# Rotary tables and latent norms moved from the end of the seven-product stage into its middle, in a hybrid mLSTM and latent-attention layer

## The chip, the cores and the metric

The kernel runs on one core of a Trainium2 chip. The metric is the time of one execution on the device in microseconds (us), as the median of several runs. TensorE (PE) does the matmuls, VectorE (DVE), ScalarE (ACT) and GpSimd (POOL) the elementwise work, and SyncE (SP) and ACT issue the DMA transfers. Each engine works through its own queue in order and waits at semaphores for the others.

## The reference

One layer with two branches that read the same normalised input, in float32, for 512 tokens of width 2048:

```
h     = rms_norm(x, norm_g)
q_a, k_a, v_a, o_a, i_a, f_a, z_a, c_q, c_kv, k_r, z_b, g_a, g_b = split(h @ w_in)
# branch A: causal conv + silu on q_a and k_a, then a gated matrix memory (mLSTM), 8 heads
y_a   = (sigmoid(o_a) * rms_norm(mlstm(q_a, k_a, v_a, i_a, f_a)) * silu(z_a)) @ w_a
# branch B: attention over low-rank latents, 16 heads of 128 + 64 (rotary) channels
q_b   = rms_norm(rms_norm(c_q, q_lat_g) @ w_uq)         # per head
k, v  = split(rms_norm(c_kv, kv_lat_g) @ w_ukv)
k_b   = rms_norm(concat(k, k_r))                        # k_r is shared by all heads
q_b, k_b: the last 64 channels turned by cos/sin(position * inv_freq)
y_b   = (causal_attention(q_b, k_b, v) * silu(z_b)) @ w_b
out   = x + (sigmoid(g_a) * y_a + sigmoid(g_b) * y_b) @ w_out
```

The latents c_q and c_kv are 512 wide each. What the change moves is the forming of the cos/sin tables, the rotary part of the shared key, and the root-mean-square norms of c_q and c_kv.

## The kernel before

**Products in split form.** Every float32 operand of a matmul is split into a high part that PE reads at its fast float32 form and a remainder. `split` does it in two instructions: ACT casts the high part, DVE subtracts it from the source (lines 104 to 106). A product then takes three matmuls: high by high, low by high, high by low.

**Stages.** (1) Three groups of columns of `w_in` are multiplied with h: the latents, the shared key and the mLSTM gates (`load_c`, `proj_tok`, `evac_c`). The raw latents are copied by ACT out of PSUM into `cc` tiles and written to DRAM (`cq_d`, `ckv_d`); 80 columns stay on the chip as `misc`. While the second and third group run, the list `later` is worked off one piece per weight tile: `build` normalises h (`normal`), splits it for the products to come (`parts`), and forms sums of its quarters (`combine`, `split_sums`). `parts` also sends the split upper half of h to DRAM (`htop_d`), two transfers on SP for each of eight row blocks: the spills.

(2) The seven-product stage (`strassen`): ten jobs of 1024 columns of `w_in` (o, z, g_a, g_b, v), each computed as a 2 x 2 block product with seven products instead of eight. A job has 28 steps, seven products (p = 0 to 6) of four, and a step is 12 matmuls. `prep` loads a weight block two steps ahead (`rx` or `rr`, SP) or subtracts two blocks (DVE, line 467), `part` splits the block one step ahead into `wh` (ACT) and `wl` (DVE, three and two buffers), `mult` issues the matmuls, and `finish` puts the output's sums into `later`, of which one piece runs per step. Outputs go through `tmp` tiles (six buffers, shared by many things) to DRAM on ACT's queue.

(3) Nine steps before the end of the last job, the pool of h's parts (`sap`) is closed, pools for the next stage are opened over it, and a generator, `early`, is advanced twice per step: it loads the raw latents back from DRAM (`latent`, `c` tiles, four loads of 512 KB), forms the rotary tables and the rotated key (`rope_setup`: about forty short DVE instructions on 128 x 128, and a dozen on POOL), then the norms of the latents (squares on ACT, inverse roots on POOL, scaling on DVE).

(4) The next stage begins with the silu gate of the first head pair (`pair_gate`, weights through `load_w`), woven with the transposes of the normalised latents into `lat`. Its weights come through `raw`, `whi` and `wlo` (4, 3 and 2 buffers). `ht`, the upper half of h, is loaded back from DRAM into the space of the stage that ends. Head pairs, mLSTM heads and output products follow.

**What sets the order.** The kernel is written as a program in one order; a planner then lists the instructions of each engine's queue by when it expects their inputs to be ready, and by program order where several are. It may put an instruction ahead of an earlier one. It inserts all semaphores. `tc.issue_after(i)` makes the instructions of a block that are on the engine of `i` stand behind `i` in the queue; `tc.add_manual_dep` does it for one instruction. Neither makes them wait for its end.

Of the kernel before, what the change touches and what calls it, by code (L numbers as in the profile page):

```python
# [19 lines left out]
P = 128  # L20
# [24 lines left out]
def hybrid_kernel(  # L45
# [207 lines left out]

    def evac_c(g):
# [50 lines left out]
    def build(j):  # L305
        f = whole[j]

# [14 lines left out]

        sums = []
# [10 lines left out]
        def split_sums():  # L334
            hi = sap.tile([P, 4, 256], F32R, tag=f"sh{j}", name=nm("sh"))
# [51 lines left out]
    def latent(i, src, gain):  # L387
# [3 lines left out]
        yield  # L391
        ss = small([P, T], "ssl")
        for t in range(T):
            A.activation(junk, c[t // 2][:, t % 2, :], AF.Square, accum_out=ss[:, t:t + 1])
        G.tensor_scalar(ss, ss, 1.0 / LORA, None, ALU.mult)
        ms = small([P, T], "msl")
        G.tensor_scalar(ms, msx, EPS, None, ALU.mult)
        G.tensor_tensor(ms, ms, ss, ALU.add)
        sc = small([P, T], "scl")
        rsqrt(sc, ms, T)  # L400
        for t in range(T):
            V.tensor_scalar(c[t // 2][:, t % 2, :], c[t // 2][:, t % 2, :], sc[:, t:t + 1], None, ALU.mult)
# [42 lines left out]
    def strassen(jobs, comb):  # L445
# [38 lines left out]
        def part(c, p, j):  # L484
# [3 lines left out]
            split(hi, lo, w)  # L488
# [60 lines left out]
        part(*steps[0])  # L549
        for n, s in enumerate(steps):  # L550
# [34 lines left out]
    def rope_setup():  # L585

        V.tensor_copy(pos_f, pos_i)
        ropes = big([P, 7, P], F32, "rope")
        angf, jq, z2, sn, cs, j4, qa = [ropes[:, a, :] for a in range(7)]
        ang = angf.rearrange("p (t f) -> p t f", t=T)  # L590
        for t in range(T):
            V.tensor_scalar(ang[:, t, :], freq, pos_f[:, t:t + 1], None, ALU.mult)
        MAGIC = 12582912.0
# [23 lines left out]
        for c in CC[1:]:  # L617
            V.scalar_tensor_tensor(cs, cs, c, z2, ALU.add, ALU.mult)
        V.tensor_scalar(cs, cs, 1.0, None, ALU.add)
# [3 lines left out]
        V.scalar_tensor_tensor(j4, j4, -4.0, jq, ALU.mult, ALU.add)  # L623
        V.tensor_tensor(qa, j4, j4, ALU.mult)
        V.tensor_scalar(qa, qa, -1.0, 1.0, ALU.mult, ALU.add)
        V.tensor_scalar(qa, qa, -1.0, None, ALU.max)
        yield
        qb = jq
        V.tensor_tensor(qb, qa, qa, ALU.mult)
        V.tensor_scalar(qb, qb, -1.0, 1.0, ALU.mult, ALU.add)  # L630
        V.tensor_tensor(qb, qb, j4, ALU.mult)
        sc_t = big([P, 2, P], F32, "rope")
        sinf, cosf = sc_t[:, 0], sc_t[:, 1]
# [6 lines left out]
        V.tensor_tensor(z2, cs, qb, ALU.mult)  # L640
        V.tensor_tensor(sinf, sn, qa, ALU.mult)
        V.tensor_tensor(sinf, sinf, z2, ALU.add)

# [12 lines left out]
        rk = big([P, 4, T, DR], F32, "rk")  # L656
        rka, rkb = rope_tables(gkr, rk[:, 0:2])

        kr, krt = rk[:, 2], rk[:, 3]
        for t in range(T):  # L660
            V.tensor_scalar(kr[:, t, :], misc[:, t, 0:64], r[:, t:t + 1], None, ALU.mult)
        for t in range(T):
            A.activation(junk[:, :DR], kr[:, t, :], AF.Square, accum_out=ssr[:, t:t + 1])
        G.tensor_tensor(krope, kr, rka, ALU.mult)
        G.tensor_tensor(krt[:, :, 0:32], kr[:, :, 32:64], rkb[:, :, 0:32], ALU.mult)
        G.tensor_tensor(krt[:, :, 32:64], kr[:, :, 0:32], rkb[:, :, 32:64], ALU.mult)
# [4 lines left out]
    def early():  # L671
        for i, (src, gain) in enumerate(((cq_d, qlg), (ckv_d, kvlg))):
            lats.append(latent(i, src, gain))
            next(lats[i])
        yield
        for _ in rope_setup():
            yield
        for lat in lats:
            next(lat)
            yield  # L680


    lats, side = [], None
    last = 28 * len(jobs) - 9
    for n, _ in enumerate(strassen(jobs, comb_h)):
        if n == last:
# [3 lines left out]
            side = early()  # L690
        if side is not None:
            for _ in range(2):
                next(side, None)
    while later:
        run_later()
    drain(side)
# [579 lines left out]
```

## Time and profile before

| | us |
|---|---|
| median of three runs (2143.95 to 2147.92) | 2143.98 |
| profiled execution, its own time | 2141.43 |
| its span, first to last instruction | 2139.7 |
| PE busy | 2105.3 (98%) |
| DVE busy | 1398.0 (65%) |
| ACT busy | 982.9 (46%) |
| POOL busy | 172.5 (8%) |

All times inside the span are us from its start. The mean granted clock of TensorE is 0.998 of full speed. Stage (1) runs to about 121.7, the seven-product stage from 124.4 to about 904, its second job from 203.6 to 279.8. Lines (L106) are those of the kernel before; L105 and L106 are the two halves of every split, so tiles tell which one it is. A busy PE is not PE at its peak, and a "<-" in brackets names what ended the idle time before an instruction.

### The profile page before, as it was taken

The numbers are of one execution on the slowest core, as the hardware profiler recorded it, in microseconds if no ns is written. First come the engines' busy times: TensorE is split into PE (matmuls) and PEld (weight loads), VectorE is DVE, ScalarE is ACT, GpSimd is POOL, SyncE is SP. The second block draws the span as 40 slices with busy tenths as digits, with TensorE's granted clock in tenths as the row PEclk, the third lists the DMA queues.
The fourth block names the chain that finished last, engine by engine and source line by source line (L and its number), as shares of the span: only waits on it lengthen the run. The fifth ranks groups of instructions, "written<-read, shape, count | busy, mean of one in ns | idle before, by whom it ended". The sixth has DMA issues, their size and how long they took to land.

```text
span 2139.7 us, 28857 instructions
## 1 busy us (share of the span) xinstructions
PE 2105.3 (98%) x10200; PEld 1781.2 (83%) x10200; DVE 1398.0 (65%) x2260; ACT 982.9 (46%) x2025; POOL 172.5 (8%) x306
## 2 busy tenths in 40 slices
PE   8999999999999999899999999999999999999999
PEld 8888888888888888688888888788878878888889
DVE  6877778787786788856666666766785433443233
ACT  8544444444444444445555555545564322222221
POOL 0000000000000000222222222201111000000000
PEclk9999999999999999999999999999999999999999
DMA  6746425524633643642222222275563543332443
GB/s 165 174 163 197 130 87 177 168 94 132 194 104 103 191 147 106 206 126 79 81 84 76 80 77 82 81 229 151 165 229 126 182 143 98 112 130 94 137 130 118
DMA packets 205313, 286.01 MB, mean 134 GB/s; under 512 B 31217, under 2 KB 111473, under 8 KB 204145
## 3 DMA queue, kind: packets, MB, share of 16 engines
q1 hardware_dynamic: 189040, 256.90, 39.6%
q10 hardware_dynamic: 16128, 27.27, 3.6%
q8 instruction: 80, 1.31, 0.3%
q14 instruction: 65, 0.52, 0.1%
HBM read 240.07 MB, written 44.04 MB: 133 GB/s over the span
## 4 chain that ended last, share of the span: by engine, by line
PE 92%; DMA 2%; DVE 2%; ACT 2%; issue 1%; POOL 1%; SPq 0%; ACTq 0%; DVEq 0%; POOLq 0%
PE acc L114 16%; PE acc L113 16%; PE acc L115 16%; PE acc L512 8%; PE acc L513 8%; PE acc L511 7%; PE aux L512 4%; PE aux L513 4%; PE aux L511 4%; PE aux L113 2%; PE aux L115 2%; PE aux L114 2%; ACT junk L236 1%; PE aux L840 1%; PE aux L800 1%
## 5 line engine op out<-in xcount | busy, mean ns | idle before, releaser
L106 DVE TENSOR_TENSOR wlo<-raw,whi 128x512 fp32r<-128x512 f32 (+3 forms) x432 | 285.4, 663 | 388.4 <-PE acc L114 279.9
L105 ACT CAST whi<-raw 128x512 fp32r<-128x512 f32 (+3 forms) x432 | 259.2, 601 | 526.5 <-PE acc L115 356.2
L106 DVE TENSOR_TENSOR wl<-rx,wh 128x1024 fp32r<-128x1024 f32 x160 | 196.6, 1229 | 114.2 <-PE aux L512 64.7
L105 ACT CAST wh<-rx 128x1024 fp32r<-128x1024 f32 x160 | 168.9, 1055 | 177.4 <-PE acc L513 106.7
L114 PE MATMUL acc<-wlo,g 128*128 128x512 f32 x512 | 200.1, 391 | 2.8 <-DVE wlo L106 2.7
L113 PE MATMUL acc<-whi,g 128*128 128x512 f32 x512 | 200.1, 394 | 2.7 <-ACT whi L105 1.6
L115 PE MATMUL acc<-whi,g 128*128 128x512 f32 x512 | 199.5, 390 | 0.8 <-DVE g L106 0.8
L105 ACT CAST wh<-rr 128x1024 fp32r<-128x1024 f32 x120 | 126.5, 1054 | 160.7 <-PE aux L513 88.1
L106 DVE TENSOR_TENSOR wl<-rr,wh 128x1024 fp32r<-128x1024 f32 x120 | 146.5, 1221 | 27.5 <-PE aux L512 14.6
L511 PE MATMUL acc<-wh,sh 128*128 128x512 f32 x400 | 155.6, 389 | 0.0
L512 PE MATMUL acc<-wl,sh 128*128 128x512 f32 x400 | 155.6, 389 | 0.0
L513 PE MATMUL acc<-wh,sl 128*128 128x512 f32 x400 | 155.6, 389 | 0.0
L114 PEld LDWEIGHTS acc<-wlo,g 128*128 128x128 f32 x512 | 96.2, 188 | 24.3 <-DVE wlo L106 5.4
L113 PEld LDWEIGHTS acc<-whi,g 128*128 128x128 f32 x512 | 95.9, 188 | 22.0 <-ACT whi L105 1.8
L115 PEld LDWEIGHTS acc<-whi,g 128*128 128x128 f32 x512 | 96.0, 188 | 21.2 <-DVE g L106 1.2
L113 PE MATMUL acc<-whi,y 128*128 128x512 f32 (+1 forms) x320 | 111.1, 348 | 0.0
L115 PE MATMUL acc<-whi,y 128*128 128x512 f32 (+1 forms) x320 | 111.0, 347 | 0.0
L114 PE MATMUL acc<-wlo,y 128*128 128x512 f32 (+1 forms) x320 | 111.0, 347 | 0.0
L113 PE MATMUL acc<-ht,whi 128*128 128x512 f32 x256 | 101.5, 397 | 0.0
L113 PE MATMUL acc<-h8h,whi 128*128 128x512 f32 x256 | 101.1, 395 | 0.0
L115 PE MATMUL acc<-h8h,wlo 128*128 128x512 f32 x256 | 100.2, 392 | 0.3 <-DVE wlo L106 0.3
L114 PE MATMUL acc<-h8l,whi 128*128 128x512 f32 x256 | 100.4, 392 | 0.0
(357 smaller groups left out, 5041.6 us busy)
## 6 DMA issues: line engine op xcount, KB each, us to landing
rr<-in_w_in SPq DMA_DIRECT2D x120, 512.0 KB, 4.8
raw<-in_w_in SPq DMA_DIRECT2D x128, 256.0 KB, 2.8
rx<-in_w_in SPq DMA_DIRECT2D x40, 512.0 KB, 5.1
raw<-in_w_b SPq DMA_DIRECT2D x64, 256.0 KB, 3.1
raw<-in_w_a SPq DMA_DIRECT2D x64, 256.0 KB, 3.0
raw<-in_w_out SPq DMA_DIRECT2D x64, 256.0 KB, 3.1
raw<-in_w_ukv SPq DMA_DIRECT2D x32, 256.0 KB, 2.8
raw<-in_w_uq SPq DMA_DIRECT2D x32, 192.0 KB, 2.4
```

The lines of the kernel that those rows point to most:

```text
L105: A.copy(dst_hi, src)
L106: return V.tensor_tensor(dst_lo, src, f32(dst_hi), ALU.subtract)
L113: PE.matmul(ps, lh, rh, start=start, stop=False)
L114: PE.matmul(ps, lh, rl, start=False, stop=False)
L115: PE.matmul(ps, ll, rh, start=False, stop=stop)
L236: A.activation(junk[:, :P], xr[:, t, :], AF.Square, accum_out=ssx[:, k, t:t + 1])
L511: PE.matmul(out[i], lh[:, tok], hi[:, n, :], start=first, stop=False, skip_group_check=cont)
L512: PE.matmul(out[i], lh[:, tok], lo[:, n, :], start=False, stop=False, skip_group_check=cont)
L513: PE.matmul(out[i], ll[:, tok], hi[:, n, :], start=False, stop=k == H8 - 1, skip_group_check=cont)
L800: PE.transpose(ps[:, t * P:(t + 1) * P], src(t), ident)
L840: PE.transpose(ps[:, j * P:(j + 1) * P], pr[:, j * P:(j + 1) * P], ident)
```

## The change

- **The first weights ahead of the copies.** The four `cc` copies of the third column group must stand behind the first `wh` cast of the seven-product stage in ACT's queue.
- **Spills later.** The two transfers to `htop_d` of a row block are issued in `split_sums`, two pieces of `later` after `parts`.
- **`rope_setup` and the norms leave the end.** From step 28 on, one piece per step of a chain is run: first `rope_setup`, cut into pieces of one to five DVE instructions, then `normalised` for c_q and for c_kv. A block around each piece queues its ACT and DVE instructions behind the latest `wh` and `wl` (`marks`). The chain must be through by nine steps before the end.
- **Borrowed storage.** The tables no longer take `big` tiles, which exist only at the end; they are formed in `rB` (the spread inverse norms, used up by then), `wg_raw` (the gate weights, used up) and the result tiles `rq` and `krope`.
- **Through DRAM.** `normalised` reads each raw latent back in pieces of 256 KB into `tmp` tiles, once for the squares and once more to scale them, and writes the scaled pieces over the raw ones. That is 16 loads and 8 stores on SP. `latent` then loads normalised values, at the same place as before, and only transposes and splits them.
- **`hold`.** The first three splits of the next stage's weights queue behind the last `wh` and `wl` on ACT and DVE.

```diff
     def split(dst_hi, dst_lo, src):
-        A.copy(dst_hi, src)
-        return V.tensor_tensor(dst_lo, src, f32(dst_hi), ALU.subtract)
+        hi = A.copy(dst_hi, src)
+        lo = V.tensor_tensor(dst_lo, src, f32(dst_hi), ALU.subtract)
+        return hi, lo
...
+    hold, marks = [0], []
+
+    def behind_parts(stack):
+        for i in marks:
+            stack.enter_context(tc.issue_after(i.ins))
...   # load_w
-                low[0] = split(hi, lo, raw)
+                with ExitStack() as held:
+                    if hold[0]:
+                        hold[0] -= 1
+                        behind_parts(held)
+                    low[0] = split(hi, lo, raw)[1]
...   # evac_c
-            A.copy(cc, ps)
+            copy = A.copy(cc, ps)
+            if g == 2:
+                copies.append(copy)
...   # build: parts, split_sums
-                SP.dma_start(htop_d[j][:, :, n:n + 256], f32(dst))
+                spills.append((htop_d[j][:, :, n:n + 256], f32(dst)))
...
         def split_sums():
+            for spill in spills:
+                SP.dma_start(*spill)
...   # latent: squares, inverse roots and scaling go
...   # strassen: part, and ahead of the steps
-            split(hi, lo, w)
+            marks[:] = split(hi, lo, w)
...
         part(*steps[0])
+        for i in copies:
+            tc.add_manual_dep(i.ins, marks[0].ins.name, in_turn, reason="first weights before the copies")
...   # rope_setup: more yields, other storage
-        ropes = big([P, 7, P], F32, "rope")
-        angf, jq, z2, sn, cs, j4, qa = [ropes[:, a, :] for a in range(7)]
+        jq, z2, sn, cs = [rB[:, a * P:(a + 1) * P] for a in range(4)]
+        angf, cosf = [wg_raw.rearrange("p k c -> p (k c)")[:, a * P:(a + 1) * P] for a in range(2)]
+        j4, qa = [rq[:, 0].rearrange("p t f -> p (t f)")[:, a * P:(a + 1) * P] for a in range(2)]
...
+    def normalised(src):
+        def piece(t):
+            x = tmp(512, "lx")
+            SP.dma_start(x, src[t // 2][:, t % 2, :])
+            return x
+        ss = small([P, T], "ssl")
+        for t in range(T):
+            x = piece(t)
             yield
+            yield
+            A.activation(junk, x, AF.Square, accum_out=ss[:, t:t + 1])
...   # ms, sc: inverse roots on POOL, as before
+        for _ in range(4):
+            yield
+        for t in range(T):
+            x = piece(t)
+            yield
+            yield
+            V.tensor_scalar(x, x, sc[:, t:t + 1], None, ALU.mult)
+            yield
+            SP.dma_start(src[t // 2][:, t % 2, :], x)
...
+    side = chain(rope_setup(), normalised(cq_d), normalised(ckv_d))
     last = 28 * len(jobs) - 9
     for n, _ in enumerate(strassen(jobs, comb_h)):
         if n == last:
             close_pool("sap")
             wpool[0] = open_pool("wp")
             big_pool.extend((None, (open_pool("bpa"), NB_A)))
-            side = early()
-        if side is not None:
-            for _ in range(2):
+            for lat in lats:
+                next(lat)
+        elif n >= 28:
+            with ExitStack() as held:
+                behind_parts(held)
                 next(side, None)
+    hold[0] = 3
     while later:
         run_later()
-    drain(side)
```

## Rows read from the trace of the kernel before

**Rows 1.** The page, engines: busy us, share of the span, instructions.
```profile
PE 2105.3 (98%) x10200; PEld 1781.2 (83%) x10200; DVE 1398.0 (65%) x2260; ACT 982.9 (46%) x2025; POOL 172.5 (8%) x306
```

**Rows 2.** Waits of PE: engine, line, releaser, us in total, times, longest us.
```profile
PE aux L512 <- DVE wl L106: 5.4, 2, 3.5
...
PE acc L511 <- ACT wh L105: 2.8, 1, 2.8
```

**Rows 3.** Windows at the start: us, busy us, granted clock, DMA share, GB/s.
```profile
121.60:126.10 4.50, 0.80 (x3) 0.30 (x2) 4.24 (x14) 3.28 (x7) 0.00 (x0) 1.00 0.65 196
126.10:130.00 3.90, 3.86 (x10) 3.04 (x11) 3.34 (x8) 1.99 (x3) 0.00 (x0) 0.56 0.97 340
```

**Rows 4.** Windows at its end; busy columns are PE, PEld, DVE, ACT, POOL.
```profile
879.60:883.20 3.60, 0.13 (x2) 0.06 (x1) 3.60 (x13) 3.44 (x13) 2.35 (x3) 1.00 0.00 0
883.20:887.30 4.10, 4.10 (x12) 3.20 (x13) 4.10 (x6) 2.44 (x7) 3.94 (x6) 0.60 0.41 128
...
892.70:902.20 9.50, 6.55 (x26) 4.21 (x25) 6.11 (x13) 2.75 (x5) 2.25 (x7) 1.00 0.62 177
902.20:924.50 22.30, 22.30 (x112) 18.57 (x113) 12.37 (x19) 9.28 (x16) 0.00 (x0) 1.00 0.78 264
```

**Rows 5.** Windows of the second job, whole, and its fourth and fifth product.
```profile
203.60:279.80 76.20, 76.20 (x338) 63.10 (x337) 58.46 (x55) 36.16 (x40) 0.00 (x0) 1.00 0.45 138
...
236.20:247.10 10.90, 10.90 (x49) 9.01 (x48) 10.90 (x11) 4.23 (x4) 0.00 (x0) 1.00 0.50 143
247.10:258.00 10.90, 10.90 (x50) 9.01 (x49) 9.06 (x10) 5.38 (x6) 0.00 (x0) 1.00 0.95 291
```

**Rows 6.** Timeline of ACT at the start: start, us, instruction, idle time before it.
```profile
120.20 0.47 ACT L258 COPY cc<-acc 128x368 f32<-128x368 f32 x1 [3.91 <-PE acc L115]
...
123.33 1.04 ACT L105 CAST wh<-rx 128x1024 fp32r<-128x1024 f32 x1
```

**Rows 7.** Timeline of SP's queue at the start (several in one row).
```profile
112.70 2.51 SPq L456 DMA_DIRECT2D rx<-in_w_in  x3
123.73 0.52 SPq L316 DMA_DIRECT2D ht<-a  x1
```

**Rows 8.** The tile rx from 100 to 136: its loads' time to landing.
```profile
DMA to landing us min/median/max: 4.3/4.7/10.8
```

**Rows 9.** Timeline of DVE at the start.
```profile
120.70 0.24 DVE L266 COPY misc<-acc 128x80 f32<-128x80 f32 x1 [2.50 <-ACT cc L258]
```

**Rows 10.** Window over the second and third column group.
```profile
55.00:118.00 63.00, 59.15 (x346) 57.07 (x347) 51.86 (x117) 33.51 (x86) 0.96 (x1) 1.00 0.69 174
```

**Rows 11.** By tile: rope (DVE, POOL), rk (DVE,ACT,POOL), c (PE,PEld,DVE,ACT), 872 to 903.
```profile
872.00:903.00 31.00, 8.68 (x41) 4.87 (x6) 0.94 0.55 181
...
872.00:903.00 31.00, 1.74 (x5) 1.39 (x8) 6.10 (x7) 0.94 0.55 181
...
872.00:903.00 31.00, 1.31 (x4) 0.55 (x4) 3.35 (x8) 5.78 (x16) 0.94 0.55 181
```

**Rows 12.** Timeline of DVE at the end.
```profile
881.62 1.47 DVE L106 TENSOR_TENSOR wl<-rx,wh 128x1024 fp32r<-128x1024 f32 x1
...
884.54 1.75 DVE L106 TENSOR_TENSOR wl<-rx,wh 128x1024 fp32r<-128x1024 f32 x1
...
900.88 1.22 DVE L106 TENSOR_TENSOR wl<-rx,wh 128x1024 fp32r<-128x1024 f32 x1
```

**Rows 13.** Timeline of SP's queue at the end.
```profile
868.80 27.53 SPq L142 DMA_DIRECT2D raw<-in_w_in  x6
896.38 15.83 SPq L705 DMA_DIRECT2D ht<-ht  x8
913.32 0.93 SPq L142 DMA_DIRECT2D raw<-in_w_in  x2
```

**Rows 14.** The latents' tiles c: their loads' time to landing.
```profile
DMA to landing us min/median/max: 4.2/5.3/7.0
```

**Rows 15.** A fifth product's step on the timeline: `wl`, and PE's first use of it.
```profile
327.03 1.22 DVE L106 TENSOR_TENSOR wl<-rr,wh 128x1024 fp32r<-128x1024 f32 x1
...
328.94 0.39 PE L512 MATMUL acc<-wl,sh 128*128 128x512 f32 x1
```

More of the change, by code (lines that the diff above doesn't have):

```diff
@@ L252, in hybrid_kernel @@
     misc = const([P, T, 80], F32, "misc")
+    in_turn = mybir.DependencyInfo(mybir.DependencyClass.NoSync, mybir.DependencyReason.DATA)
+    copies = []
     def evac_c(g):
@@ L306, in build @@
         f = whole[j]
+        sums, spills = [], []
         def normal():
@@ L321, in parts @@
             hN[H8 + j] = (hi, lo)
-        sums = []
         def combine():
@@ L390, in latent @@
             SP.dma_start(c[n], src[n])
[L391 to L402, printed above, removed]
         yield
@@ L618, in rope_setup @@
             V.scalar_tensor_tensor(cs, cs, c, z2, ALU.add, ALU.mult)
+            yield
         V.tensor_scalar(cs, cs, 1.0, None, ALU.add)
@@ L623, in rope_setup @@
         V.scalar_tensor_tensor(j4, j4, -4.0, jq, ALU.mult, ALU.add)
+        yield
         V.tensor_tensor(qa, j4, j4, ALU.mult)
         V.tensor_scalar(qa, qa, -1.0, 1.0, ALU.mult, ALU.add)
+        yield
         V.tensor_scalar(qa, qa, -1.0, None, ALU.max)
-        yield
         qb = jq
         V.tensor_tensor(qb, qa, qa, ALU.mult)
+        yield
         V.tensor_scalar(qb, qb, -1.0, 1.0, ALU.mult, ALU.add)
         V.tensor_tensor(qb, qb, j4, ALU.mult)
-        sc_t = big([P, 2, P], F32, "rope")
-        sinf, cosf = sc_t[:, 0], sc_t[:, 1]
+        yield
+        sinf = angf
         sin_t = sinf.rearrange("p (t f) -> p t f", t=T)
@@ L640, in rope_setup @@
         V.tensor_tensor(z2, cs, qb, ALU.mult)
+        yield
         V.tensor_tensor(sinf, sn, qa, ALU.mult)
         V.tensor_tensor(sinf, sinf, z2, ALU.add)
+        yield
         def rope_tables(g, tab):
@@ L655, in rope_setup @@
         yield
-        rk = big([P, 4, T, DR], F32, "rk")
-        rka, rkb = rope_tables(gkr, rk[:, 0:2])
-        kr, krt = rk[:, 2], rk[:, 3]
+        rka, rkb = rope_tables(gkr, rB.rearrange("p (n t f) -> p n t f", n=2, t=T))
+        yield
+        kr, krt = krope, wg_raw.rearrange("p k c -> p (k c)").rearrange("p (t f) -> p t f", t=T)
         for t in range(T):
             V.tensor_scalar(kr[:, t, :], misc[:, t, 0:64], r[:, t:t + 1], None, ALU.mult)
+        yield
         for t in range(T):
             A.activation(junk[:, :DR], kr[:, t, :], AF.Square, accum_out=ssr[:, t:t + 1])
+        G.tensor_tensor(krt[:, :, 0:32], kr[:, :, 32:64], rkb[:, :, 0:32], ALU.mult)
+        yield
+        G.tensor_tensor(krt[:, :, 32:64], kr[:, :, 0:32], rkb[:, :, 32:64], ALU.mult)
+        yield
         G.tensor_tensor(krope, kr, rka, ALU.mult)
-        G.tensor_tensor(krt[:, :, 0:32], kr[:, :, 32:64], rkb[:, :, 0:32], ALU.mult)
-        G.tensor_tensor(krt[:, :, 32:64], kr[:, :, 0:32], rkb[:, :, 32:64], ALU.mult)
         yield
@@ L669, in rope_setup @@
         yield
[L671 to L676, printed above, removed]
+    def normalised(src):
[6 more added lines that the diff above has]
+            x = piece(t)
             yield
-        for lat in lats:
-            next(lat)
             yield
-    lats, side = [], None
+            A.activation(junk, x, AF.Square, accum_out=ss[:, t:t + 1])
+        G.tensor_scalar(ss, ss, 1.0 / LORA, None, ALU.mult)
+        ms = small([P, T], "msl")
+        G.tensor_scalar(ms, msx, EPS, None, ALU.mult)
+        G.tensor_tensor(ms, ms, ss, ALU.add)
+        sc = small([P, T], "scl")
+        rsqrt(sc, ms, T)
+        for _ in range(4):
+            yield
+        for t in range(T):
+            x = piece(t)
+            yield
+            yield
+            V.tensor_scalar(x, x, sc[:, t:t + 1], None, ALU.mult)
+            yield
+            SP.dma_start(src[t // 2][:, t % 2, :], x)
+    side = chain(rope_setup(), normalised(cq_d), normalised(ckv_d))
+    lats = [latent(i, src, gain) for i, (src, gain) in enumerate(((cq_d, qlg), (ckv_d, kvlg)))]
     last = 28 * len(jobs) - 9
@@ L689, in hybrid_kernel @@
             big_pool.extend((None, (open_pool("bpa"), NB_A)))
-            side = early()
-        if side is not None:
-            for _ in range(2):
+            for lat in lats:
[3 more added lines that the diff above has]
+                behind_parts(held)
                 next(side, None)
+    assert next(side, None) is None
+    hold[0] = 3
     while later:
         run_later()
-    drain(side)
     for n in reversed(STP):
```

## The prediction, made before the change was run

> **What bounds the kernel now.** The page comes first: TensorE is busy 98% of the span [rows 1], so a change that leaves its matmuls alone can only win back time in which PE stands still or runs at half clock. The list of waits, cut to PE, says where to look: the longest, and one more near the top, are waits for `wl` and `wh`, the split weights of the seven-product stage [rows 2]. The windows put them at that stage's two ends. At its start PE works 0.80 of 4.50 us, and then has 3.90 us at a granted clock of 0.56 [rows 3]; at its end it works 0.13 of 3.60 us, then has 4.10 us at 0.60, and after a full stretch works 6.55 of 9.50 us [rows 4]. In between PE is full, 76.20 of 76.20 us in the second job [rows 5]. Those two ends are all that this change can gain, apart from a little in the stage before.
>
> What they cost: at the start 3.70 us of idle and 0.44 x 3.90 = 1.72 of clock, 5.4 together. At the end 3.47 + 2.95 = 6.4 of idle and 0.40 x 4.10 = 1.6 of clock, 8.0. Both half-clock stretches come right after a standstill of over 3 us; the waits from 892.70 to 902.20 are shorter, and the granted clock stays 1.00 there [rows 4]. So the clock term goes when the long waits go, and stays with them.
>
> **Part 1, the start: the first weights ahead of the copies.** ACT sits idle 3.91 us until 120.20, does four `cc` copies and a cast, and turns to the first `wh` at 123.33 [rows 6]. That weight's load was issued at 112.70 [rows 7] and such loads land after 4.7 us in the median [rows 8], so at 117.4. With the copies put behind it on ACT, the cast (1.04 us) runs from about 117.5 to 118.6. It needs its buffer too: `rra`, `rx` and `wl` take 56 of the 64 KB that `hp` leaves, so one of the three 4 KB buffers of `wh` lies beyond the h tiles that PE still reads, and I take it that the first cast gets it. DVE is idle for 2.50 us until 120.70 [rows 9], so `wl` (1.22 us) is done by 120, before the last old product ends at 121.6, and PE steps from one stage into the next. The copies run from 120.2 as today, since PE frees their banks only then. If the load took the 10.8 us of the slowest [rows 8], copies and PE would wait until 124.6, some 0.2 us later than today.
>
> What is late next is the second step's `wl`: from 120.70 on DVE works off the copies of `misc`, the first lines of the gates and the last `combine`, and all of that stays; in 121.60 to 126.10 it is busy 4.24 of 4.50 us [rows 3]. I leave 0.9 us of PE waiting there and expect no half-clock stretch. Gain 4.5 us; bounds -0.2 and 5.4.
>
> The spills of `parts`, issued two pieces later, belong here. SP gets its third `rx` load out by 115.2 and then nothing before a spill at 123.73, with the next `rx` and all `rr` loads behind it [rows 7]. PE doesn't wait for those today; 4.5 us earlier it would come close, and the moved spill gets them ahead. In 55 to 118, where the other spills stand among the weight loads, PE idles 63.00 - 59.15 = 3.85 us [rows 10], some of it for weights that SP issued late. I take 0.3 gained; bounds -1 and 2.
>
> **Part 2, the end: rotary tables and norms taken out.** DVE spends 8.68 us on the rotary tile, another 1.2 on the key's (1.74 less 0.54 counted in both) and 3.35 on scaling the latents [rows 11]; POOL is busy in all three of the bad windows [rows 4]. This stands ahead of weights: the `wl` that PE lacks from 879.6 starts at 881.62, at the end of the rotary chain, and the stage's last one waits behind the scalings until 900.88 [rows 12]. Without them DVE has here the `wl`s, the output splits, eight latent splits and the next product's weights. Those could take their place, but `hold` puts the first three of the next stage's splits behind the last `wh` and `wl`. The four remaining steps of 2.72 us are then continuous. From 902.20 to 924.50 the same latent splits and products run today with PE full and DVE busy 12.37 of 22.30 us [rows 4]. I leave 0.7 of waiting. Gain 7.3; bounds 2 (rival A) and 8.0.
>
> What is issued next also counts. SP stands from 868.80 to 896.3 in six `raw` loads, the last of them, as I read it, waiting for buffers that the next stage's `wlo` splits free; the eight `ht` loads start at 896.38 and two more `raw` follow them [rows 13]. With the first `wlo` right behind the last `wl`, two steps after 879.6 and so at 885 or 886, this queue moves some 9 us earlier, PE 7 to 8. The latents' loads stay where they are, and land 4.2 to 7.0 us after issue [rows 14]; their transposes wait for them alone.
>
> **Part 3, the middle: the same work spread over steps 28 to 106.** A step is 76.20 / 28 = 2.72 us. DVE is busy 58.46 of 76.20 us in the job of steps 28 to 55 [rows 5]: room for 17.7 us, and the rotary work needs 8.68 + 1.2 = 9.9. The room is uneven. In that job's fourth product DVE is busy 10.90 of 10.90 us, in the fifth 9.06 [rows 5], and in such a stretch a `wl` that ends at 328.25 is read at 328.94 [rows 15], 0.7 us to spare. Those eight steps get one or two short instructions each, 13 of some 0.2 us (8.68 / 41), 2.5 us in all, so DVE ends them 0.7 us behind and catches up in the next product. Steps 58 to 106 get eight scalings of 0.42 us on DVE, eight squares on ACT, which is busy 36.16 of 76.20 us [rows 5], and on SP 24 transfers of 256 KB: 6.3 MB, at the 264 GB/s of 902 to 924 [rows 4] 24 us over 133, where DMA stands at 0.45 [rows 5]. I charge 0.6 us; bounds 0 and 15 (all moved DVE work, 13.2, on PE's path, and 1.8 for POOL beside it).
>
> For POOL: next to it a `wl` took 1.75 us [rows 12] instead of 1.22 [rows 15], 0.5 lost, within the 0.7 to spare. The Trainium skill (SBUF — State Buffer, Who interferes with whom) speaks against this move: a DVE instruction with two SBUF inputs, which `wl` is, and a GpSimd instruction that reads SBUF shut each other out, and the second waits until the first has ended. By that rule `wl` could lose all of POOL's time, 2.35 + 3.94 + 2.25 us in the windows of rows 4, and the sum would be some 8 us worse. The trace agrees that they disturb each other, not that `wl` loses that much.
>
> **The sum.** -4.5 - 0.3 - 7.3 + 0.6 = -11.5 us. The profiled execution took 2141.43 us (span 2139.7 and 1.7 around it), which would become 2129.9; the median of the three timed runs is 2.55 higher, so 2143.98 - 11.5 = 2132.5.
>
> **Rivals.**
> A: the reload takes the end's place. If the fifth `raw` stays late, so does the queue behind it, and PE comes to its last `raw`s 6 us too early. For it: SP's queue is in order, and DMA stands at 0.78 there [rows 4]. Against it: `hold` lets that `wlo` come before 886. End gain 2: 2143.98 - 4.5 - 0.3 - 2 + 0.6 = 2137.8.
> B: the start's wait is only exchanged, DVE's backlog delaying `wl` as ACT delayed `wh` [rows 3]. Start gain 1: 2136.0. Against it: DVE's idle time before 120.70 [rows 9].
> C: both, or the ordering doesn't do what it says: 1 at the start, 2 at the end, and 1 lost in the middle: 2141.7, no difference.
> D, slower: a scaling on DVE waits for its piece. It is queued two steps, 5.4 us, after the load, and DVE's queue is in order. The latents' loads, twice the size, landed after 4.2 to 7.0 us [rows 14], and a piece whose `tmp` buffer (six, shared with the outputs) comes late lands later still. From 5.4 + 0.7 us on (0.7 to spare [rows 15]) PE stops; at 9.5 us, my estimate for 7.0 and a buffer that is 2.5 late, it stops for 3.4 us, with up to 1.7 of clock after it. Three such pieces of the eight bring 2132.5 + 15.3 = 2147.8, four 2152.9, and I put it at 2153. Against it: pieces of 256 KB, and PE without one wait in this stage today.
>
> **How the numbers follow.** Forecast 0.50, A 0.14, B 0.12, C 0.16, D 0.08. A measurement of this kernel can tell about 0.2% from no change, 4.3 us. The forecast and B lie beyond it and A mostly (0.12), so faster 0.74; C and the rest of A, 0.18, are within it; slower 0.08. The low end: all good bounds, -5.4 - 2 - 8.0, give 2128.6, and 1 us for the spread of the runs 2127.5. The high end takes in A and half of C, 2141; D and the rest of C stay out.
>
> **What would show it.** Part 1: the first `wh` cast ahead of the four `cc` copies, PE idle near 121.7 for under 1 us, no half-clock stretch near 126. Part 2: no rotary line and no scaling after 864, PE idle from 879 to 903 under 1 us, the fifth `raw` and `ht` issued some 9 us earlier; if they still come at 894, it is A. Part 3: POOL busy between 205 and 290, PE full in each job from 203 to 432; a PE wait for `wl` there, or DVE waiting for a piece, is D. A time above 2139.7 makes the forecast wrong.

## The result, and the profile after

| us | before | after |
|---|---|---|
| median of the timed runs | 2143.97 (2139.12 to 2147.92, 4 runs) | 2129.92 (2127.49 to 2130.97, 4 runs) |
| ratio, with its 95% interval | 1 | 0.9934 (0.9911 to 0.9956) |
| profiled execution, its own time | 2141.43 | 2130.97 |
| its span | 2139.7 | 2129.0 |

The forecast of 2132.5 us was 2.6 us too high, inside its range. First the page's line of engines, which answers to [rows 1]:

```profile
PE 2100.9 (99%) x10200; PEld 1780.4 (84%) x10200; DVE 1397.0 (66%) x2260; ACT 982.9 (46%) x2025; POOL 173.6 (8%) x306
```

The work is the same, 10200 matmuls and 2260 instructions on DVE; PE is busy 4.4 us less. PE's waits, by line, releaser, us in total, times and longest, answer to [rows 2]:

```profile
PE acc L115 <- DVE wlo L106: 6.5, 6, 2.0
PE acc L114 <- ACT whi L105: 5.3, 3, 2.1
...
PE acc L518 <- DVE wl L106: 0.5, 1, 0.5
```

The 5.4 us for `wl` at the stage's end and the 2.8 for `wh` at its start are gone; 0.5 us for `wl` is left at the start. What stands at the head now, `wlo` and `whi`, belongs to stage (1) and to the last products, which the change hardly touches. The windows of the stage's start, its end and its second job with the job's fourth and fifth product (us, busy PE, PEld, DVE, ACT, POOL, granted clock, DMA share, GB/s) answer to [rows 3 to 5]; the job begins 3.4 us earlier than before:

```profile
119.00:123.11 4.11, 4.11 (x26) 4.11 (x25) 2.38 (x6) 1.94 (x3) 0.00 (x0) 1.00 1.05 394
123.11:130.00 6.89, 6.37 (x28) 4.86 (x28) 5.91 (x14) 4.22 (x7) 0.00 (x0) 1.00 0.95 309
870.00:885.80 15.80, 15.80 (x72) 13.06 (x71) 9.23 (x11) 6.85 (x10) 0.00 (x0) 1.00 1.01 345
885.80:911.15 25.35, 25.35 (x128) 21.04 (x127) 12.25 (x19) 10.82 (x18) 0.00 (x0) 1.00 0.64 213
...
200.20:276.40 76.20, 76.20 (x338) 63.12 (x337) 66.14 (x101) 37.54 (x48) 6.87 (x10) 1.00 0.47 142
232.80:243.70 10.90, 10.90 (x50) 9.01 (x48) 10.90 (x15) 4.23 (x4) 0.00 (x0) 1.00 0.61 171
243.70:254.60 10.90, 10.90 (x50) 9.03 (x49) 10.88 (x18) 5.38 (x6) 0.00 (x0) 1.00 0.81 263
```

At the start PE stands 0.52 us in all, at the end not at all, and the granted clock is 1.00 in all of these windows. In the second job DVE is busy 7.7 us more, the fifth product is as full as the fourth, and PE is as full as before.

Medians of this kernel scatter by 2 us between sets of runs (the experiments show it), so parts are measured by PE's own milestones, each read from one profile. The third and fourth column tell of the change; the ninth-last step is where the work at the end used to begin. `pr` holds the probabilities of the attention, `g` the inputs of the last products.

| us | stage (1) ends at | to the stage's ninth-last step | to the first transposes of `pr` | to the products of `g` | to PE's last matmul of the output | sum |
|---|---|---|---|---|---|---|
| before | 121.67 | 742.88 | 116.82 | 594.45 | 560.17 | 2135.99 |
| after | 123.28 | 737.85 | 106.87 | 594.27 | 563.07 | 2125.34 |
| difference | +1.61 | -5.03 | -9.95 | -0.18 | +2.90 | -10.65 |

The change's two places gave 15.0 us. In this execution 4.5 us of that were lost where the change moves next to nothing: in stage (1), whose end lies anywhere from 119.7 to 124.4 in the eleven profiles of this study that have it unchanged, and in the last products. In the latter PE waited 2.00 us for a `whi`, and half clock followed:

```profile
1580.37:1583.50 3.13, 1.13 (x6) 0.95 (x6) 1.14 (x2) 1.88 (x7) 0.00 (x0) 1.00 1.01 365
1583.50:1587.00 3.50, 3.50 (x11) 2.72 (x10) 2.98 (x5) 2.57 (x5) 0.00 (x0) 0.51 0.62 214
```

### The profile page after: what moved, and what is told of

Read it like the earlier page. It is cut to its first block, busy times and chain, and to the rows that moved or that the text cites. A ratio compares the mean times of both kernels' runs of the same rounds, so it can differ in the third digit from the quotient of the medians.

```text
span 2129.0 us, 28895 instructions
## 1 busy us (share of the span) xinstructions
PE 2100.9 (99%) x10200; PEld 1780.4 (84%) x10200; DVE 1397.0 (66%) x2260; ACT 982.9 (46%) x2025; POOL 173.6 (8%) x306
## 3 DMA queue, kind: packets, MB, share of 16 engines
q8 instruction: 80, 1.31, 0.3%
## 4 chain that ended last, share of the span: by engine, by line
PE 93%; DMA 2%; ACT 2%; DVE 1%; issue 1%; POOL 0%; SPq 0%; ACTq 0%; DVEq 0%; POOLq 0%
PE acc L115 16%; PE acc L116 16%; PE acc L114 16%; PE acc L518 8%; PE acc L519 8%; PE acc L517 8%; PE aux L519 4%; PE aux L518 4%; PE aux L517 4%; PE aux L114 2%; PE aux L116 2%; PE aux L115 2%; ACT junk L248 1%; PE aux L883 1%; PE aux L843 1%
```

## The experiments

All were timed in five rounds. A ratio is to the kernel before, run on the same chip (its medians there: 2141.1 to 2143.2). "The step" is the third column of the table above, "the end" the fourth.

**The copies first again.**

```diff
-        for i in copies:
-            tc.add_manual_dep(i.ins, marks[0].ins.name, in_turn, reason="first weights before the copies")
```

> The changed kernel (2129.9 us), but without the order at the start: the four cc copies need not stand behind the first wh cast. Theory (the copies ahead of the cast were what PE waited for): near 122 to 126 PE stands 3 to 4 us for wh and wl again, a stretch at half clock follows, and the time is 2133.5 to 2135.5, some 4 to 5.5 us more than the changed kernel. Rival B (DVE's backlog sets the first wl anyway): PE stands under 1 us, as in the changed kernel, or stands 3 us with the order too; time within 1 us of 2129.9. The end (868 to 925, shifted by the loss) keeps PE without a gap either way.

2134.31 us, ratio 0.9959 (0.9946 to 0.9973). ACT's timeline, first of this kernel, then of the changed one, shows the order that was taken away; the windows are those of this kernel's start:

```profile
125.18 0.47 ACT L273 COPY cc<-acc 128x368 f32<-128x368 f32 x1 [0.57 <-ACT cc L273]
...
126.05 1.04 ACT L105 CAST wh<-rx 128x1024 fp32r<-128x1024 f32 x1
```

```profile
118.95 1.05 ACT L105 CAST wh<-rx 128x1024 fp32r<-128x1024 f32 x1 [1.05 <-DMA rx<-in_w_in]
121.81 0.97 ACT L273 COPY cc<-acc 128x368 f32<-128x368 f32 x2 [1.81 <-PE acc L116]
```

```profile
124.38:128.90 4.52, 1.27 (x4) 0.54 (x3) 4.26 (x14) 3.30 (x7) 0.00 (x0) 0.73 0.70 210
128.90:133.30 4.40, 4.40 (x11) 3.43 (x12) 3.39 (x9) 1.91 (x3) 0.00 (x0) 0.50 1.09 350
```

The standstill (3.25 us) and the half clock are back, the step takes 743.33 us, 5.5 more than in the changed kernel. The theory holds; rival B's claim, that DVE would set the first weight anyway, falls.

**The spills early again.**

```diff
-                spills.append((htop_d[j][:, :, n:n + 256], f32(dst)))
+                SP.dma_start(htop_d[j][:, :, n:n + 256], f32(dst))
...
-            for spill in spills:
-                SP.dma_start(*spill)
```

> The changed kernel, but the spills to htop_d are issued in parts again, two pieces earlier; the order of the first weights stays. Theory of the prediction: the last spill stands on SP ahead of the fourth rx and all rr loads, so they come out near 123.7 instead of 116.5, PE then lacks a weight near 130 for 1 to 3 us, and stage (1) idles at 54 and 69 as much as the kernel before or a little less; time 2130 to 2133. Rival 1 (the spills are indifferent): rx and rr late, but PE without a wait over 0.7 us from 122 to 140, time within 1 us of 2129.9. Rival 2 (the moved spills themselves delay the raw loads of stage (1)): the gaps at 54 and 69 shrink from 2.03 and 2.14 to the 0.72 and 0.87 of the kernel before, stage (1) ends 1.5 us earlier, time near 2128.5.

2127.91 us, ratio 0.9931 (0.9916 to 0.9945), the step 737.85. Rival 1 is nearest, for a reason that none named: in the traces of this run and of the changed kernel each engine's queue holds the same instructions in the same order, wherever the two lines stand in the program. Beside the new order on ACT the edit is nothing, and the 2.0 us between this median and 2129.92 are the scatter of one and the same program. What moved the last spill is the new order on ACT in part: with it, three `rr` loads stand ahead of the spill (here, in the changed kernel and in the run with the start alone, below), without it (the run above) one. In the kernel before, the fourth `rx` and all `rr` stood behind it [rows 7]; why the run above has two of these loads ahead of it is not shown.

**No hold.**

```diff
-    hold[0] = 3
+    hold[0] = 0
```

> The changed kernel, but the first three splits of the next stage's weights may stand anywhere in the queues of ACT and DVE (hold taken away). Theory (hold is needed for the end's gain): these splits come ahead of the last wh and wl, PE stands 1 to 3.5 us between 870 and 895, perhaps with a half-clock stretch; time 2131 to 2135. Rival (taking out the rotary chain and the scalings was enough, the planner orders the splits by their inputs and these come late): PE without a gap over 0.7 us from 870 to 925, time within 1 us of 2129.9.

2127.74 us, ratio 0.9932 (0.9918 to 0.9946). Two `wlo` now stand between the last four `wl`, and the end takes 106.86 us, as with hold. PE stands nowhere from 870 to 925. The rival is right: in the changed kernel hold gains nothing. Its time, 2.2 us below 2129.92, is close to the 2127.91 of the run above.

**The start alone, and with hold.** The kernel before with the first weights ahead of the copies and the late spills; then hold added to it.

> The kernel before with the change's start (first weights ahead of the copies, spills later) and its hold (first three splits of the next stage behind the last wh and wl), but with the rotary tables and the norms at the end as in the kernel before. Theory (the work itself, not the order of the next stage's splits, made the waits at the end): PE stands 3 to 3.5 us for a wl near 880 with half a clock's loss after it, and 2 to 3 us in short waits until 905; at the start it stands under 1 us; time 2143 less the start's 4.5 to 6: 2136 to 2139.5. Rival (hold alone repairs the end): gaps between 870 and 910 sum to under 2 us, time 2130 to 2133.

> The kernel before with the change's start alone: first weights ahead of the copies, spills later; rotary tables and norms at the end and no hold, as in the kernel before. With the start and hold together the start's gain was seen (PE stands 0.53 us at 124 instead of 3.74) and the whole still took 2142.5 us, as much as the kernel before. Theory H (hold took it: with the scalings still ahead of the last wl, it sends the next stage's first wlo behind them and leaves PE no other work between 888 and 896): without hold the end costs what it costs in the kernel before, about 6.4 us of idle time and 1.7 of clock, and the time is 2142.0 less 4.5 to 5.5: 2136.5 to 2138.5. Rival P (the end is paced by POOL's and ACT's chain from the nineteenth-last instruction on, and PE coming early only waits longer): idle time between 868 and 905 is 8 to 10 us here too, a second stretch at half clock stands there, and the time is 2140.5 to 2143.

The start alone: 2137.05 us, ratio 0.9981 (0.9972 to 0.9990); the step takes 737.86, the end 118.50. With hold: 2142.46 us, ratio 1.0002 (0.9993 to 1.0011); 737.98 and 122.10. Waits of PE for `wl` and `wh` in the stage, the first with hold, the second without:

```profile
PE aux L530 <- DVE wl L106: 6.0, 2, 4.4
PE aux L529 <- ACT wh L105: 2.3, 1, 2.3
```

```profile
PE aux L521 <- DVE wl L106: 5.4, 2, 3.5
...
PE aux L520 <- ACT wh L105: 0.3, 1, 0.3
```

And the windows of the end with hold:

```profile
877.40:882.10 4.70, 4.70 (x11) 3.73 (x12) 4.21 (x6) 2.62 (x8) 4.54 (x7) 0.50 0.75 222
888.80:892.40 3.60, 0.91 (x4) 0.43 (x4) 0.26 (x1) 2.94 (x6) 1.81 (x5) 1.00 0.68 221
892.40:899.20 6.80, 5.13 (x12) 3.54 (x13) 4.67 (x8) 0.86 (x2) 0.45 (x3) 0.50 0.62 231
```

What was expected of the run with hold, 2136 to 2139.5, failed: it took hold to be harmless. Of the two accounts given afterwards theory H holds and P falls: without hold PE's idle time at the end is 6.6 us, nearly that of the kernel before (6.4), and with it 8.9. As long as the norms stand ahead of the last `wl`, the next stage's first products are what PE does meanwhile; hold takes them away and PE stands longer. A second stretch at half clock, P's sign, stands in both runs, but with hold the two stretches last 6.8 us each, without it 3.4. Hold cost 3.6 us in the profiles and, by the ratios, 0.21%, 4.5 us. So hold, which gains nothing in the changed kernel, would have been a loss without the move.

**Which half of the move gained the end.** Only the norms back at the end; only the rotary work back at the end, first free, then held behind the latest weights:

```diff
-    side = chain(rope_setup(), normalised(cq_d), normalised(ckv_d))
+    side = chain(normalised(cq_d), normalised(ckv_d))
...
+        if n >= last:
+            with ExitStack() as held:
+                behind_parts(held)
+                for _ in range(8):
+                    next(side, None)
```

> The changed kernel, but the norms of the latents stand at the end again, run by run as in the kernel before (raw latents loaded to c, squares, inverse roots and scalings two pieces per step from nine steps before the end); the rotary tables stay in the middle, hold and the order at the start stay. Theory (the waits at 892 to 902 of the kernel before were the scalings' and the squares', 2.95 us in six waits): PE stands 1.5 to 3 us in short waits in the 12 us around the stage's end and none at some 866; time 2131.5 to 2133 beside 2127 to 2130 for the changed kernel. Rival (the rotary chain, which pushed everything later, was behind both groups of waits): PE without a gap over 0.7 us from 865 to 925, time within 1 us of the changed kernel; the norms' 24 transfers and 8 scalings in the middle were then for nothing.

> The changed kernel, but the rotary tables and the rotated key are formed at the end, eight short pieces per step from nine steps before the end; the norms stay in the middle, hold and the order at the start stay. Theory (the 41 DVE instructions of the rotary tile, 8.68 us, were what delayed the wl at 879.6): PE stands 2 to 3.5 us for a wl near 865 to 872, a half-clock stretch follows, 3.5 to 5.2 in all; time 2131.5 to 2134 beside 2127 to 2130. Rival (the long wait came of both chains together, and DVE carries one of them): PE without a gap over 0.7 us, time within 1 us of the changed kernel.

> The changed kernel, but the rotary tables are formed at the end, eight pieces per step from nine steps before the end, each held behind the latest wh and wl (the run with the rotary work at the end and no such hold let it slip to the start of the stage); 35 of the DVE instructions then stand between the 273rd and the 276th of the stage's 280 wl. The norms stay in the middle. Theory (in the kernel before, the chain of short instructions, some of which wait for POOL, stands whole between two wl and delays the second): held and cut, it stands between three wl; DVE loses 8.7 us over three steps of 2.72 us with 0.7 to 1.7 us of margin each, so PE stands 2 to 4 us near 860 to 875, perhaps with a stretch at half clock; time 2131 to 2134.5 beside 2127 to 2130. Rival (spread over three steps and without the scalings it is hidden): no PE gap over 0.7 us, time within 1 us of the changed kernel, and moving it to the middle was not needed.

Norms at the end: 2129.39 us, ratio 0.9943 (0.9930 to 0.9955), the end 111.46 us. Rotary work held at the end: 2131.76 us, 0.9953 (0.9941 to 0.9966), the end 110.02. So the norms alone cost 4.6 us of the 9.95, and the rotary work alone 3.2, together 2.2 less than both at once; both theories hold, though the first put the time 2 us too high. Their waits, the norms' first; a `wl` each time, behind scalings that wait for POOL, and behind the rotary chain:

```profile
878.57 1.67 DVE L420 TENSOR_SCALAR c<-c,scl 128x512 f32<-128x512 f32 x4 [1.45 <-POOL scl L125]
880.16 1.21 DVE L106 TENSOR_TENSOR wl<-rx,wh 128x1024 fp32r<-128x1024 f32 x1
...
PE aux L530 <- DVE wl L106: 2.2, 2, 1.8
```

```profile
PE aux L518 <- DVE wl L106: 2.6, 1, 2.6
```

The free one (2128.23 us, 0.9941, 0.9929 to 0.9953) tested something else than meant. Nothing held the tables at the end, and their storage is free early; the planner ran the tables in stage (1), most of them from 108.5 on, and DVE came late to the seven-product stage's first weight:

```profile
120.47 0.54 DVE L669 SCALAR_TENSOR_TENSOR rB<-wg_raw,gkr 128x128 f32<-128x128 f32 x1
120.93 1.47 DVE L106 TENSOR_TENSOR wl<-rx,wh 128x1024 fp32r<-128x1024 f32 x1
```

PE waits for that one 1.80 us, and the step takes 740.39, 2.5 more. The end is 106.88, which says nothing of rotary work at the end.

**The chain in the middle without its marks.**

```diff
-            with ExitStack() as held:
-                behind_parts(held)
-                next(side, None)
+            next(side, None)
```

> The changed kernel, but the pieces in the middle need not stand behind the latest wh and wl (issue_after taken from the chain; hold stays). Theory (the place in DVE's queue matters little where DVE has 0.65 us and more to spare before each wl): least distance from the end of a wl to PE's first use of it falls from 0.65 to 0.2 to 0.6 us, PE has no wait over 0.3 us from 140 to 860, time within 1 us of the changed kernel, 2127 to 2130. Rival (short DVE instructions waiting for POOL stand ahead of weights without the marks): PE stands 0.5 to 2 us in some of the steps between 203 and 290, sum 2 to 6 us, time 2131 to 2135.

2133.36 us, ratio 0.9962 (0.9948 to 0.9976); the step 744.60, 6.75 more. 3.8 of it lie before the second job (the tables slipped into stage (1) here too), and 2.9 in the third and fourth, where in each a scaling that waits for POOL stands ahead of weights; this is the fourth's:

```profile
368.69 0.49 DVE L717 TENSOR_SCALAR lx<-lx,scl 128x512 f32<-128x512 f32 x1 [2.64 <-POOL scl L125]
...
370.23 1.22 DVE L106 TENSOR_TENSOR wl<-rx,wh 128x1024 fp32r<-128x1024 f32 x1
```

The marks are what makes the middle free. The theory's 0.3 us was wrong, the rival's mechanism right, at another place than it named.

**The scaling right behind its load.**

```diff
             x = piece(t)
-            yield
-            yield
             V.tensor_scalar(x, x, sc[:, t:t + 1], None, ALU.mult)
```

> The changed kernel, but each scaling of a latent piece in the middle is queued in the same step as the load of its piece, instead of two steps (5.4 us) later; all eight then wait for their transfer. Rival D's mechanism, made to happen: such loads land 2.1 to 6.9 us after issue, DVE stands that long in each of eight scalings, and PE has 0.65 to 1.5 us to spare, so PE stands 1 to 6 us in most of the eight steps from about 88 to 106; sum 8 x 4 = 32 us with up to 1.7 us of clock after each standstill of over 3 us: 2150 to 2170. If DVE's waits are covered (the planner puts the next wl ahead of the waiting scaling, or the load lands before DVE comes to it), PE stands nowhere over 1 us in 270 to 420 and the time stays within 2 us of 2129.9, and D was never a danger.

2126.69 us, ratio 0.9929 (0.9915 to 0.9942); the step 738.58, 0.7 more. One scaling of the eight waits:

```profile
323.73 0.49 DVE L715 TENSOR_SCALAR lx<-lx,scl 128x512 f32<-128x512 f32 x1 [1.32 <-DMA lx<-cq]
```

PE stands 0.4 us for the `wl` after it; the 2150 to 2170 expected did not come. The other seven loads had landed 1.3 us and more before their scaling: in the queues a load may stand well ahead of its place in the program. So the two steps between it and its use there are not what keeps rival D away.

**More work on DVE in the middle.** Two extra instructions per step on a tile that nothing else uses.

```diff
+                if n < 107:
+                    for _ in range(2):
+                        V.tensor_tensor(pad, pad, pad, ALU.max)
```

> The changed kernel with extra work: two more in-place DVE instructions on a 128 x 168 tile, about 0.25 to 0.3 us each, with every piece of the middle (steps 28 to 106, 79 steps, together 40 to 47 us). Theory (room in the middle is a job's DVE time: 76.2 - 58.5 = 17.7 us, the rotary work uses 9.9 of it and the extra 14 to 17): in the second job DVE's work comes to 82 to 85 us, PE stands 6 to 9 us for wl there, and about nothing in the third and fourth, where the scalings take 1.7 each; time 2134 to 2139. Rival (the planner moves idle room along, or the extra falls in gaps of DVE): PE stands under 2 us in all from 203 to 430, time 2127 to 2131. Second rival (each stretch with DVE already full pays by itself, 8 steps of each job x 0.55 less the 0.65 to spare): 4 us in each of the three jobs, 12 in all, 2139 to 2142.

2131.64 us, ratio 0.9953 (0.9940 to 0.9965). Jobs two to four take 78.50, 78.43 and 76.71 us instead of 76.16 each, 5.2 in all, for 158 instructions of 0.31 us and more, 49 us. The theory is wrong in its sizes: 2.3 us in the second job, not 6 to 9, and as much again in the third. DVE is busy 78.47 of the second job's 78.50 us, so its room was used up there, but the instruction behind an extra one often starts 0.25 us after it, so each cost less than its 0.31. The first rival has the standing time nearly right, 2.06 us from 203 to 430, but the loss is 5.2, the rest of it in matmuls that count as busy; the granted clock is 1.00 there. The second rival's 12 us are far off. How much DVE work the middle still takes for nothing lies between the changed kernel's and this run's, and is not settled further.

**The start's rule elsewhere.**

```diff
+            if gates and k == 3:
+                tc.add_manual_dep(middle[3].ins, first.ins.name, in_turn, reason="weights before the last copy")
...
-            dg = tmp(P, "diag")
+            dg = diags[:, t * P:(t + 1) * P]   # in rq
...   # gqn, gkn, mgh and cw are loaded from the tenth step of the seven-product stage on
+        if n > 8 and late_loads:
+            with tc.issue_after(loads[0].ins):
+                SP.dma_start(*late_loads.pop(0))
```

> The changed kernel, with what its start taught applied to the three waits that are left in stage (1): the fourth cc copy of the second column group, which waits for its tmp buffer at 91 us with the next weights' casts behind it, must stand behind the third group's fourth whi cast; the four diag tiles of the inverse norms take rq's space instead of tmp buffers, for which DVE waits at 54 us with wlo behind it; and seven small loads that are used much later (the conv weights among them, 5 us on SP between 57 and 66) are issued in the seven-product stage. Theory: the PE gaps at 54, 69 and 92 (0.8 to 2.0, 0.8 to 2.1 and 1.1 to 2.3 in the runs so far) fall below 0.7 each, stage (1) ends 2.5 to 4 us earlier, time 2124 to 2126.5 beside 2127 to 2130. Rival (these waits are transfers that land late whatever the order): the gaps stay within their range so far, time 2127 to 2130; the late small loads could also cost a wait of 1 to 2 us near 130 to 160.

2122.36 us (2121.91 to 2122.91), ratio 0.9912 (0.9898 to 0.9925): the lowest median of all, and below the forecast for it, 2124 to 2126.5. The changed kernel's own interval (0.9911 to 0.9956) touches this one, so the gain over it rests on the profiles: stage (1) ends at 118.20, earlier than in any other run and 5.1 us earlier than in the changed kernel's profile; step (737.85) and end (106.83) are as there. Another 2.9 us between the two profiles lie in the last products, where none of the three edits acts. Which of the three gave how much was not separated.

PE's wait at 69 is gone, the one at 92 is 0.31 us. The one at 54 now stands at 51.64 and takes 1.31 us, not under 0.7. The diag tiles no longer wait for buffers, but the first two wait for POOL's inverse root, and a `wlo` stands behind them on DVE:

```profile
51.96 0.48 DVE L320 TENSOR_SCALAR rq<-ident,r 128x128 f32<-128x128 f32 x2 [2.91 <-POOL r L125]
52.36 0.54 DVE L106 TENSOR_TENSOR wlo<-raw,whi 128x368 fp32r<-128x368 f32 x1
```

## Why the prediction was right, and where it was not

**The sum.** It was -11.5 us; the two places gave -15.0, of which the profiled execution kept 10.65 and the medians 14.05. That the time came within 2.6 us is luck in part: the gain was put too low, and this set of runs lay a little high. The same queues gave 2127.91 in another, 4.6 below the forecast.

**Part 1, 4.5 us.** Right in mechanism and size: 5.03 with the middle in it, 5.02 with the start alone, 5.5 when taken back. `wh` is cast at 118.95 and PE waits 0.52 us, less than the 0.9 left for it. The first cast did not find DVE's backlog in its way. But it could have: where the rotary tables slipped ahead of it, PE waited 1.80 us, which is rival B, made by another chain.

The 0.3 us for the spills was wrong as a step: beside the new order on ACT the edit changes no queue.

**Part 2, 7.3 us: the term that was mis-sized.** It measured 9.95, above its upper bound of 8.0. PE's idle time there was 6.42 us between the two milestones, all gone, as forecast. The 0.7 us of waiting that the forecast left there did not come. And PE's busy time for the same matmuls fell by 3.53 us, where the forecast had 1.6 for the clock and nothing else: 1.9 us were left out. The stretch at half clock in the kernel before, and the timelines, first of the kernel before, then of the changed one:

```profile
884.00:887.40 3.40, 3.40 (x10) 2.63 (x9) 3.40 (x5) 1.68 (x6) 3.32 (x4) 0.50 0.50 154
...
885.57 0.63 PE L511 MATMUL aux<-wh,h8h 128*128 128x512 f32 x1
886.00 0.63 PE L512 MATMUL aux<-wl,h8h 128*128 128x512 f32 x1
...
892.96 1.52 PE L407 MATMUL aux<-ident,c 128*128 128x128 f32 x4 [0.21 <-DVE c L402]
```

```profile
885.16 0.39 PE L518 MATMUL aux<-wl,h8h 128*128 128x512 f32 x1
885.39 0.40 PE L519 MATMUL aux<-wh,h8l 128*128 128x512 f32 x1
885.62 0.60 PE L413 MATMUL aux<-ident,c 128*128 128x128 f32 x4
```

At half clock the matmuls stand 0.43 us apart instead of 0.23. That is the 1.6 us of the forecast, and it was right. Of the 1.9 left out, 1.08 lie in the 32 transposes of `c`: the first four, each of which waits for its scaling, take 1.52 us instead of 0.60. Another 0.55 lie in the stage's own matmuls outside the half-clock stretch, 0.11 in each of three that come right after a wait. The rest, 0.3, is in the next products. The bound of 8.0 failed because it took a busy PE to be PE at its peak, which it wasn't where operands came late.

One reading behind the clock term was wrong. The half clock at the start does not follow one standstill of over 3 us but two waits, of 2.76 and 0.98; the runs with shorter waits are below.

The credit given to hold was wrong: without it the end is the same to 0.01 us, and beside the old end it is a loss of 4.5 us. What made the four last steps continuous is that no rotary chain and no scaling stands ahead of their `wl`; each of the two alone brought a wait back, so both halves of the move were needed.

Of the queue behind, `ht` is issued from 876.25 on, 20 us earlier instead of the 9 forecast; the fifth `raw` is not earlier (893.36, before 894.76), since the planner now puts all of `ht` ahead of it:

```profile
865.38 8.68 SPq L150 DMA_DIRECT2D raw<-in_w_in  x4
876.25 11.89 SPq L748 DMA_DIRECT2D ht<-ht  x8
893.36 3.82 SPq L150 DMA_DIRECT2D raw<-in_w_in  x4
```

That time was named as the sign of rival A. The sign was bad, for `raw` was never needed sooner: PE stands nowhere from 885.8 to 911.2.

**Part 3, 0.6 us lost.** It cost nothing: 737.85 with all of the moved work in the middle, 737.86 without. The fourth product is as full as before, and the smallest distance from a `wl` to its first use, 0.67 us in steps 28 to 106 before, is 0.65; DVE does not fall the 0.7 us behind there that the forecast allowed. The room was there, and the marks kept it for the weights: without them it was a loss.

POOL's price fell on POOL. Here one of its multiplications starts 0.15 us after a `wl`, and takes 1.44 us where its twin took 0.56 and 0.45 are usual; `wl` took 1.27 instead of 1.22:

```profile
261.57 0.56 POOL L667 TENSOR_TENSOR rq<-wg_raw,gqr 128x128 f32<-128x128 f32 x1 [199.30 <-DVE wg_raw L659]
...
262.93 1.44 POOL L667 TENSOR_TENSOR rB<-wg_raw,gkr 128x128 f32<-128x128 f32 x1
```

```profile
262.78 1.27 DVE L106 TENSOR_TENSOR wl<-rx,wh 128x1024 fp32r<-128x1024 f32 x1 [0.97 <-PE acc L518]
```

In the kernel before it was the `wl` that came second, at 884.54, 0.59 us after an instruction on POOL, and it took 1.75 [rows 12]:

```profile
883.95 1.27 POOL L664 TENSOR_TENSOR krope<-rk 128x256 f32<-128x256 f32 x1
```

The Trainium skill (SBUF — State Buffer, Who interferes with whom) says that the order of issue, and not the shape, decides which of the two is held up. The rows of both kernels agree. In the forecast its rule was weighed as if `wl` always came second.

**The rivals.** A did not come. B exists, as said, but not in the changed kernel. C's time came about, within 1 us, in the run of the start with hold on the old end: a gain at the start given back at the end. D did not come, and queueing each scaling with its load raised it only to one wait of 1.32 us.

## What to carry to other kernels

Where one product's results leave through the engine that also prepares the next product's weights, put the first weights ahead of the copies: it paid 5 us at one seam here, and in the last run, with two other edits, the wait at another fell from 1.1 to 2.3 us to 0.31. Slack in the middle of a stage was free here only for work that is held behind the weights in the queues; a planner that may choose ran the same instructions over 90 us early, ahead of a weight. Measure an edit by the stage that it acts in, and first see whether it changed any queue: here one changed none, and one, hold, cost nothing or 4.5 us by what stood beside it.

## What the runs showed of the hardware

The granted clock falls after shorter waits than [rows 4] had suggested, and not every time. After nearly the same wait for the stage's last `wl`, 1.94 and 1.95 us, one kernel's clock stayed at 1.00 and another's fell to 0.50 a little over a microsecond later, the first of these rows from the kernel before, the second from the run with the start alone:

```profile
903.30:906.70 3.40, 3.40 (x21) 2.78 (x19) 2.00 (x5) 1.21 (x2) 0.00 (x0) 1.00 1.07 367
```

```profile
896.30:899.70 3.40, 3.40 (x12) 2.71 (x11) 1.46 (x4) 0.62 (x1) 0.00 (x0) 0.50 1.05 405
```

In the same 3.40 us PE did 21 matmuls at 2.4 GHz and 12 at 1.2 GHz. In the run with the rotary work held at the end a wait of 1.33 us in stage (1) was followed by half clock, and the one of 2.55 us for `wl` was not. So the length of a wait alone did not tell, what else decides is not shown, and a term for the clock after a wait of 1.3 to 2.6 us is a chance.

POOL can be shut out far longer than one instruction. In the run with more work on DVE, a multiplication that takes 0.45 us elsewhere took 9.72:

```profile
260.14 9.72 POOL L667 TENSOR_TENSOR rq<-wg_raw,gqr 128x128 f32<-128x128 f32 x1 [199.82 <-DVE wg_raw L659]
269.82 0.46 POOL L668 TENSOR_TENSOR rq<-wg_raw,gqr 128x128 f32<-128x128 f32 x1
```

```profile
268.32 1.22 DVE L106 TENSOR_TENSOR wl<-rx,wh 128x1024 fp32r<-128x1024 f32 x1
269.46 1.71 DVE L679 TENSOR_SCALAR krope<-misc,r 128x64 f32<-128x64 f32 x4
```

From 260.14 on DVE runs one instruction with two inputs after another without a pause, and POOL ends 0.4 us after DVE has come to one that reads a single tile and a scalar, at 269.46. The same run has a second case, an instruction on 128x4 that took 0.28 us elsewhere in it:

```profile
370.26 10.88 POOL L705 TENSOR_SCALAR ssl<-ssl 128x4 f32<-128x4 f32 x1 [64.06 <-ACT junk L704]
```

DVE is busy all that time, again with two-input instructions, and POOL's instruction ends at 381.14, just after the first gap between two of DVE's (0.03 us, at 381.05). That the one held up the other is read from these times alone. In such a stretch DVE's slack is POOL's too.
